# Attention on one core: product 5 of weights and V split into seven smaller products, product 2 split in two of four periods only

## The chip, the cores and the metric

The kernel runs on one core of one Trainium2 chip. The metric is the device time of one execution in microseconds (us); lower is better.

## The reference

For each of 8 batches, with q, k and v of 2048 x 512 in float32:

```python
scores = np.matmul(q, k.transpose(0, 2, 1)) / np.sqrt(d_k)
attn_weights = special.softmax(scores, axis=-1).astype(np.float32)
return np.matmul(attn_weights, v)
```

## The kernel before

**Two products, both by a seven-product scheme.** Both large products (q with k, and the weights exp(scores) with v) are cut into 2 x 2 blocks and made with seven block products in place of eight (the Strassen-Winograd form). The block sums that this needs are additions on VectorE. Operands are float16, sums on TensorE are float32 in PSUM. The softmax has no maximum; exp is taken on ScalarE straight from PSUM, and the row sums come out of an extra column of ones beside v (257 columns in place of 256), so that each output is scaled by a reciprocal at the end.

**Stages.** The work is 32 periods g = 0 to 31, four to each batch; I call g mod 4 the quarter 0 to 3. A period has 28 slots. In each slot one product of q and k is made for the queries of the next two periods (`Group.product`, two matmuls of 512 columns, L317), and between them stand the products of the weights with v for the period's own 2 x 128 query pairs, the "pair" a and the pair b (`Pair.product`, eight matmuls of 256 or 257 columns, L414). The table `ORDER` (L558) says after which slot which product of weights and v stands: "a5" at 10 is product 5 of pair a, "a7'" product 7 of the pair a of the period before. The periods 0, 30 and 31 have orders of their own (`FIRST`, `ALONE`, `LAST`).

**Products 1 and 2 are split once more.** For pairs a and b together, product 1 ("s1" to "s4" in the table) and product 2 ("t1" to "t4") are cut again into seven products of four matmuls with 128 columns each (`fine`, L519). They need sums of weights (`a_sums`, L494 to L497, in the tiles `si`) and of v (`vi_sums`, L241 to L244, once a batch, in `ti`), and within the chain one ScalarE copy of 256 columns from one PSUM bank to another (L527), two ScalarE copies of 128 columns to the output tile (L530, L534) and two VectorE additions (L536, L541). Each later stage ("s2" after "s1") writes columns that the copy has to have read.

**Sums.** `p_sums` (L368 to L371) makes four sums of 128 x 1024 for each pair of a period; a and b have tiles of their own, two buffers each. In the even periods pair a's sums are cut in two (6 of 8 blocks, then 2). `k_sums`, `q_sums` and `v_sums` make the sums of k, q and v for what comes next. `sums_of` (L615) and `KSUMS` (L592) place all of them by slot.

**Outputs.** Each half of a pair's output is a tile of 128 x 512 float32 from a pool of six. ScalarE scales one part (L423), VectorE adds another (L426), and when both 256-column halves are done one DMA of 256 KB stores it from SyncE's queue (L433). The same queue carries the DMA transposes of q and k (L150), in program order. `prefetch` (L601) issues them and the loads.

**Order.** Nothing is scheduled by a tool: every engine works through its instructions in the order in which the program names them, and semaphores hold back what is not ready. Of PSUM's eight banks the pools `qx` (2), `qy`, `qz` (1 each) hold the scores, `px` and `pz` (2 each) the products of weights and v.

Of the kernel before, what the change touches and what calls it, by code (L numbers as in the profile page):

```python
# [12 lines left out]
def kernel(  # L13
# [22 lines left out]
    P = 128  # L36
# [30 lines left out]
    spool = ctx.enter_context(tc.tile_pool(name="spool", bufs=2))  # L67
    opool = ctx.enter_context(tc.tile_pool(name="opool", bufs=6))
# [35 lines left out]
    si = {n: const.tile([P, NI, P], F16, name=f"si{n}") for n in (1, 2, 4)}  # L104
    ti = {}
# [124 lines left out]
    def t3_inner(b):  # L230
        return vi_blocks(b + 1 if b + 1 == B else b)[1]

    def vi_sums(b, s):
        b11, b12, b21, b22 = vi_blocks(b)
        if not ti:
            for n in (1, 2, 4):
                ti[n] = ipool.tile([P, 2, NI, P], F16, tag=f"t{n}", name=f"ti{n}")[:]
        ti[3] = t3_inner(b)
        at = lambda x: x[:, s]
        return [  # L240
            lambda: sub(at(ti[1]), at(b12), at(b11)),  # L241
            lambda: sub(at(ti[2]), at(b22), at(ti[1])),
            lambda: sub(at(ti[3]), at(b22), at(b12)),
            lambda: sub(at(ti[4]), at(b21), at(ti[2])),  # L244
        ]
# [109 lines left out]
    def p_sums(g, which, j0=0, j1=NJ):  # L355

        left, right = pts[g // 2]
        if (g, which) not in psums:
            psums[g, which] = [
                spool.tile([P, NJ, P], F16, tag=f"s{n}", name=f"s{n}") for n in (1, 2, 4)  # L360
            ]
        s1, s2, s4 = psums[g, which]
        cols = columns(g, which)
        js = slice(j0, j1)
        a11, a21 = left[0][:, js, cols], right[:, js, 0, cols]
        a12, a22 = left[1][:, js, cols], right[:, js, 1, cols]
        return [
            lambda: add(s1[:, js], a21, a22),  # L368
            lambda: sub(s2[:, js], s1[:, js], a11),
            lambda: sub(a21, a11, a21),  # L370
            lambda: sub(s4[:, js], a12, s2[:, js]),  # L371
        ]

# [3 lines left out]

    class Pair:

        def __init__(self, g, which):
            self.g, self.which, self.done = g, which, 0

        def product(self, n, j0=0, j1=NJ):
            g = self.g
            left, right = pts[g // 2]
            s1, s2, s4 = psums.get((g, self.which), (None,) * 3)
# [4 lines left out]
            self.apart = g == NP - 1 and alone  # L393
            if n == 1 and j0 == 0:
                self.x = bank("px")
            elif n == 2:
                self.y = bank(own + "y")
            elif n == 5:
                self.z = bank(own + "z")
            lhs, rhs, dst = {  # L400
                1: (lambda j: left[0][:, j, cols], lambda j: vh[:, j, 0, 0:H], "x"),
                2: (lambda j: left[1][:, j, cols], lambda j: vh[:, j, 1, 0:H], "y"),
# [7 lines left out]
            width = H + 1 if n in (3, 5) else H  # L410
            first = n in (1, 2, 5)
# [18 lines left out]
        def store(self, o, half, ds=slice(0, D)):  # L430
            b, sp = divmod(self.g // 2, NSP)
            n = (2 * sp + half) * NT + self.g % 2 * 2 + "ab".index(self.which)
            nc.sync.dma_start(out=out[b, n * P:(n + 1) * P, ds], in_=o[:, ds])  # L433

        def store_first(self):
            self.done += 1
            if self.done == 2:
                self.store(self.o1, 0)

        def after5(self):  # L440
            self.o2 = opool.tile([P, D], F32, tag="o")
            self.r2 = small.tile([P, 1], F32, tag="r2")
            nc.vector.reciprocal(out=self.r2[:], in_=self.z[:, H:H + 1])  # L443
            self.scaled(self.o2[:, H:D], self.z[:, 0:H], self.r2)

        def after3(self):
            self.o1 = opool.tile([P, D], F32, tag="o")
            self.r1 = small.tile([P, 1], F32, tag="r1")
            nc.vector.reciprocal(out=self.r1[:], in_=self.z[:, H:H + 1])
            self.scaled(self.o1[:, 0:H], self.x[:, 0:H], self.r1)  # L450

        def after2(self):
            self.final(self.o1[:, 0:H], self.y[:, 0:H], self.r1)
            self.store_first()

        def after6(self):
            self.scaled(self.o1[:, H:D], self.x[:, 0:H], self.r1)
            self.final(self.o1[:, H:D], self.z[:, 0:H], self.r1)
            self.store_first()

        def after7(self):
            self.final(self.o2[:, H:D], self.x[:, 0:H], self.r2)
            if self.apart:
                self.store(self.o2, 1, slice(H, D))

        def after4(self):
            self.scaled(self.o2[:, 0:H], self.x[:, 0:H], self.r2)
            self.store(self.o2, 1, slice(0, H if self.apart else D))

    class Fine(Pair):  # L470

        def after3(self):
            self.o1 = opool.tile([P, D], F32, tag="o")
            self.r1 = small.tile([P, 1], F32, tag="r1")
            nc.vector.reciprocal(out=self.r1[:], in_=self.z[:, H:H + 1])
            self.scaled(self.o1[:, H:D], self.z[:, 0:H], self.r1)
            self.scaled(self.o1[:, 0:H], self.x[:, 0:H], self.r1)

        def after6(self):
            self.final(self.o1[:, H:D], self.x[:, 0:H], self.r1)
            self.store_first()

    def a_blocks(g, s):
        left = pts[g // 2][0][s]
        ca, cb = columns(g, "a"), columns(g, "b")
        lo, hi = slice(0, NI), slice(NI, NJ)
# [11 lines left out]
    def fine(g, s, stage):  # L500

        a11, a12, a21, a22 = a_blocks(g, s)
        b11, b12, b21, b22 = vi_blocks(g // NQT)
        pa, pb = (pairs.setdefault((g, w), Fine(g, w)) for w in "ab")
        if stage == 1:
            for p in (pa, pb):
                if s == 0:
                    p.x = bank("px")
                else:
                    p.y = bank("pz")  # L510
        xa, xb = (pa.y, pb.y) if s else (pa.x, pb.x)

        def product(n, dst):
            lhs, rhs = {
                1: (a11, b11[:, s]), 2: (a12, b21[:, s]), 3: (si[4], b22[:, s]), 4: (a22, ti[4][:, s]),
                5: (si[1], ti[1][:, s]), 6: (si[2], ti[2][:, s]), 7: (a21, t3_inner(g // NQT)[:, s]),
# [6 lines left out]

        if stage == 1:
            product(1, xb[:, 0:P])
            product(5, xb[:, P:H])
            nc.scalar.copy(out=xa[:, 0:H], in_=xb[:, 0:H])  # L527
        elif stage == 2:
            product(6, xb[:, 0:P])
            nc.scalar.copy(out=pa.o2[:, 0:P], in_=xb[:, 0:P])  # L530
            product(2, xa[:, 0:P])
        elif stage == 3:
            product(7, xb[:, 0:P])
            nc.scalar.copy(out=pa.o2[:, P:H], in_=xb[:, 0:P])  # L534
            product(3, xa[:, P:H])
            nc.vector.tensor_add(xa[:, P:H], xa[:, P:H], pa.o2[:, 0:P])  # L536
            if s:
                pa.after2()
        else:
            product(4, xb[:, 0:P])  # L540
            nc.vector.tensor_add(xb[:, P:H], xb[:, P:H], pa.o2[:, P:H])  # L541
            if s:
                pb.after2()
# [3 lines left out]
    def pv(g, which):  # L547
        if which[0] in "st":
            return fine(g, "st".index(which[0]), int(which[1]))
# [12 lines left out]
    FIRST = "a1< b1< a1> a5 b1> a3 a2 a6 - b5 - b3 b2 b6".split()  # L562
    ALONE = "a7' b7' a4' b4' a1 a5 b1 a3 b5 a6 b3 a2 a7 b6 a4 b2".split()
    LAST = "b7' a1 b4' a5 b1 a3 b5 a6 b3 a2 b6 a7 b7 a4 b2 b4".split()
# [4 lines left out]
    def after_slot(g):  # L569
        order = {0: FIRST, NP - 2: ALONE, NP - 1: LAST}.get(g)  # L570
        if order is None:
            return ORDER
        return {2 * n + 1: x for n, x in enumerate(order) if x != "-"}

    PLAN = {}
    for qt_, slot_, *what_ in (
# [13 lines left out]
    KSUMS = {  # L592
        divmod(slot, NS): (c, n)
        for c, slots in (
            (0, (39, 42, 43, 44)), (1, (56, 59, 60, 65)), (2, (67, 71, 74, 76)), (3, (84, 86, 88, 90))
        )
        for n, slot in enumerate(slots)
    }
    background = deque()

    def prefetch(g, slot):  # L601
# [9 lines left out]
        if (qt, slot) in KSUMS and b + 1 < B:  # L611
            c, n = KSUMS[qt, slot]
            k_sums(c)[n]()

    def sums_of(g, slot):  # L615

        if g == 0:
            return [first_sum(x) for x in SUMS0.get(slot, "").split()]
        todo = []
        b, qt = divmod(g, NQT)  # L620
        inner = g < NP - 2

        def put(slots, items):
            todo.extend(f for at, f in zip(slots, items) if at == slot)

        sp = g // 2 + 1
        if g % 2 == 0 and sp < NP // 2:
            put((2,), q_sums(sp)[2:])
        if g % 2 == 1 and sp + 1 < NP // 2:
            put((24, 26), q_sums(sp + 1))  # L630
        if g % 2 == 0:
            put((4, 4, 5, 5), p_sums(g, "a", NE))
        if inner:
            put((6, 7, 11, 12), a_sums(g, 0))
            put((14, 17, 21, 22), a_sums(g, 1))
        if g % 2 == 0 and sp < NP // 2:
            put((7,), q_sums(sp)[3:])
        put((8, 9, 10, 13) if inner else (7, 9, 11, 13), p_sums(g, "b"))
# [221 lines left out]
```

## Time and profile before

| What | Value |
|---|---|
| Time, median of 3 runs | 795.77 us (795.51 to 795.99) |
| Time of the profiled execution | 795.86 us |
| Its span, first to last instruction | 793.8 us |
| TensorE matmuls (PE) busy | 787.4 us, 99% of the span |
| VectorE (DVE) busy | 678.0 us, 85% |
| ScalarE (ACT) busy | 608.4 us, 77% |
| GpSimd (POOL) busy | 72.3 us, 9% |
| Granted TensorE clock | 1.000 |

The profile has one execution. Its own time is 2.06 us above its span. Rows of it name a line of the kernel, the engine, the operation, output and inputs and shapes; "busy" is the time in which at least one instruction of the engine ran, so that the durations of overlapping instructions add up to more.

### The profile page before, as it was taken

To read this page: it belongs to the slowest core of one execution; us is meant where nothing else is said; L and a number is where in the kernel's file an instruction comes from. 1 tells how busy PE (TensorE), PEld (TensorE's weight loads), DVE (VectorE), ACT (ScalarE), POOL (GpSimd) and SP (SyncE) were. 2 spreads that over 40 slices of the span, in tenths; PEclk is the share of its full clock that TensorE was granted. 3 is DMA by queue.
4 is the path that set the end of the run, shared out by engine and by line. 5 is a ranking of instruction groups with operands and counts; after the bars stand their busy time and mean duration, and the time that the engine had idled before them with its cause. 6 is when DMAs were issued, how large, how long until landed. Compare 5 with 4: busy or idle time off the path is not lost.

```text
span 793.8 us, 16565 instructions
## 1 busy us (share of the span) xinstructions
PE 787.4 (99%) x6226; PEld 537.0 (68%) x6226; DVE 678.0 (85%) x1568; ACT 608.4 (77%) x1194; POOL 72.3 (9%) x106
## 2 busy tenths in 40 slices
PE   9999999999999999999999999999999999999998
PEld 6556666666666666666666666666666666666677
DVE  3789889979899898998989888898888989889773
ACT  4678777877877887778787788878778777778852
POOL 4011010001100010001100111001110101000000
PEclk9999999999999999999999999999999999999999
DMA  9989997989938999389994799667995879911112
GB/s 221 181 147 143 151 179 151 161 136 205 194 65 162 160 200 184 83 152 150 201 163 107 150 152 214 123 135 140 169 206 97 159 137 188 182 41 41 54 55 106
DMA packets 188160, 115.96 MB, mean 146 GB/s; under 512 B 122288, under 2 KB 170800, under 8 KB 188080
## 3 DMA queue, kind: packets, MB, share of 16 engines
q0 software_dynamic: 49648, 49.29, 43.1%
q1 hardware_dynamic: 138144, 65.29, 39.0%
q8 instruction: 48, 0.79, 0.4%
q10 hardware_dynamic: 288, 0.33, 0.1%
q14 instruction: 32, 0.26, 0.1%
HBM read 100.73 MB, written 33.55 MB: 169 GB/s over the span
## 4 chain that ended last, share of the span: by engine, by line
PE 96%; DMA 2%; ACT 1%; DVE 1%; issue 0%; ACTq 0%
PE t L317 45%; PE t L414 36%; PE t L519 11%; PE t L260 2%; DMA kraw<-stage 2%; PE tr L160 1%; PE tr L137 0%; PE t L728 0%; PE t L276 0%; ACT left L253 0%; DVE o L426 0%; ACT o L423 0%; ACT right L253 0%; DVE kraw L163 0%; DVE cz L342 0%
## 5 line engine op out<-in xcount | busy, mean ns | idle before, releaser
L317 PE MATMUL t<-qraw,kraw 128*128 128x512 f16 x728 | 206.4, 379 | 0.1
L414 PEld LDWEIGHTS <-s 128*128 128x128 f16 x1536 | 149.7, 97 | 58.8 <-issue 0.5
L253 ACT ACTIVATE left<-t 128x512 f16<-128x512 f32 (+1 forms) x260 | 156.1, 603 | 22.3 <-PE t L317 16.7
L423 ACT ACTIVATE o<-t,r 128x256 f32<-128x256 f32 x256 | 116.4, 486 | 59.7 <-DVE r L443 32.9
L253 ACT ACTIVATE right<-cz 128x1024 f16<-128x1024 f32 x122 | 129.5, 1061 | 10.0 <-DVE cz L339 9.7
L317 PE MATMUL t<-qs,ks 128*128 128x512 f16 x488 | 135.2, 379 | 0.0
L414 PE MATMUL t<-vt,s 128*128 128x257 f16 (+1 forms) x1024 | 133.8, 273 | 0.0
L414 PEld LDWEIGHTS <-right 128*128 128x128 f16 x1024 | 100.2, 98 | 37.2 <-issue 0.5
L317 PEld LDWEIGHTS <-kraw 128*128 128x128 f16 x976 | 90.3, 98 | 44.3 <-issue 0.6
L426 DVE SCALAR_TENSOR_TENSOR o<-t,r,o 128x256 f32<-128x256 f32 x192 | 92.2, 481 | 27.0 <-PE t L414 11.9
L333 ACT COPY cz<-t 128x512 f32<-128x512 f32 x120 | 70.4, 587 | 47.2 <-PE t L317 45.0
L339 DVE TENSOR_TENSOR cz<-t,cz 128x512 f32<-128x512 f32 x122 | 83.7, 686 | 22.2 <-PE t L317 21.6
L519 PEld LDWEIGHTS <-left 128*128 128x128 f16 x928 | 68.9, 98 | 41.1
L342 DVE TENSOR_TENSOR cz<-t,cz 128x512 f32<-128x512 f32 x122 | 83.8, 687 | 14.6 <-PE t L317 8.3
L317 PEld LDWEIGHTS <-ks 128*128 128x128 f16 x732 | 66.5, 97 | 39.4 <-issue 0.2
L328 ACT COPY t<-t 128x512 f32<-128x512 f32 x120 | 69.0, 575 | 19.2 <-PE t L317 14.9
L317 PE MATMUL t<-qs,kraw 128*128 128x512 f16 x244 | 72.5, 379 | 0.0
L317 PE MATMUL t<-qraw,ks 128*128 128x512 f16 x244 | 72.5, 378 | 0.0
L336 ACT COPY cz<-t 128x512 f32<-128x512 f32 x122 | 71.4, 585 | 0.0
L519 PE MATMUL t<-vh,left 128*128 128x128 f16 x696 | 67.4, 219 | 0.0
L414 PE MATMUL t<-vh,s 128*128 128x257 f16 x512 | 66.9, 272 | 0.2 <-ACT o L423 0.2
L414 PE MATMUL t<-vt,right 128*128 128x256 f16 x512 | 66.2, 273 | 0.3 <-DVE o L426 0.3
(85 smaller groups left out, 937.7 us busy)
## 6 DMA issues: line engine op xcount, KB each, us to landing
out_dram<-o SPq DMA_DIRECT2D x127, 256.0 KB, 3.0
vh<-in_v_dram POOLq DMA_DIRECT2D x32, 512.0 KB, 11.8
stage<-in_q_dram POOLq DMA_DIRECT2D x28, 512.0 KB, 8.2
stage<-in_k_dram POOLq DMA_DIRECT2D x28, 512.0 KB, 7.7
right<-in_q_dram POOLq DMA_DIRECT2D x2, 512.0 KB, 10.2
right<-in_k_dram POOLq DMA_DIRECT2D x2, 512.0 KB, 12.3
first<-in_q_dram SPq DMA_DIRECT2D x2, 256.0 KB, 3.5
cz<-in_q_dram SPq DMA_DIRECT2D x2, 256.0 KB, 4.8
```

The lines of the kernel that those rows point to most:

```text
L253: nc.scalar.activation(out=out_, in_=in_, func=EXP, scale=inv_sqrt_d)
L260: nc.tensor.matmul(st[:], kops[c][0][:, n, dc, :], qraw[0][:, half * NT:(half + 1) * NT, dc, :], start=(dc == 0), stop=(dc == ND - 1),)
L317: nc.tensor.matmul(dst[:], lhs[:, j, dc, :], rhs[:, :, dc, :], start=(n in (1, 5) and dc == 0), stop=(dc == 1), skip_group_check=True,)
L328: f(out=self.y[:], in_=self.x[:])
L333: f(out=self.cz[:, 1, :], in_=self.z[:])
L336: nc.scalar.copy(out=self.cz[:, 0, :], in_=self.x[:])
L339: nc.vector.tensor_add(self.cz[:, 1, :], self.x[:], self.cz[:, 1, :])
L342: nc.vector.tensor_add(self.cz[:, 0, :], self.z[:], self.cz[:, 0, :])
L414: nc.tensor.matmul(dst[:, 0:width], lhs(j), rhs(j), start=(first and j == 0), stop=(j == NJ - 1), skip_group_check=True,)
L423: nc.scalar.activation(out=out_, in_=src, func=COPY, scale=r[:])
L426: nc.vector.scalar_tensor_tensor(out=out_, in0=src, scalar=r[:], in1=out_, op0=MULT, op1=ADD)
L519: nc.tensor.matmul(dst, lhs[:, j, :], rhs[:, j, :], start=(n == 1 and j == 0), stop=(j == NI - 1), skip_group_check=True,)
```

## The change

The core of the diff (new names of variables and the parts that only follow from these are left out):

```diff
-    spool = ctx.enter_context(tc.tile_pool(name="spool", bufs=2))
-    opool = ctx.enter_context(tc.tile_pool(name="opool", bufs=6))
+    spool = ctx.enter_context(tc.tile_pool(name="spool", bufs=1))
+    opool = ctx.enter_context(tc.tile_pool(name="opool", bufs=7))
...
+    ui = {n: const.tile([P, NI, P + 2 if n == 1 else P], F16, name=f"ui{n}") for n in (1, 2, 4)}
+    ti3 = const.tile([P, NI, P], F16, name="ti3")
+    ci = const.tile([P, 2, P], F32, name="ci")
...
     def p_sums(g, which, j0=0, j1=NJ):
-                spool.tile([P, NJ, P], F16, tag=f"s{n}", name=f"s{n}") for n in (1, 2, 4)
+                spool.tile([P, NJ, 2 * P], F16, tag=f"s{n}", name=f"s{n}") for n in (1, 2, 4)
...
-    ORDER = {
-        1: "a7'", 3: "b7'", 5: "a4'", 7: "b4'", 8: "s1", 10: "a5", 11: "s2", 13: "b5", 14: "s3",
-        16: "a3", 17: "s4", 18: "b3", 20: "a6", 21: "t1", 23: "t2", 24: "b6", 25: "t3", 27: "t4",
-    }
+    INNERS = ("xz", "xyz", "xyz", "xz")
+    PRODUCTS = (
+        "a7'@1 b7'@2 a4'@6 u1@8 b4'@9 u2@9 s1@12 u3@12 s2@13 u4@14 s3@15 a3@15 s4@16 b3@18 a6@20 "
+        "a2@22 b6@24 b2@27",
+        "a7'@1 b7'@3 a4'@5 u1@7 b4'@10 u2@10 s1@11 u3@12 s2@13 u4@14 s3@15 a3@16 s4@17 b3@18 "
+        "a6@20 t1@21 t2@23 b6@24 t3@25 t4@27",
+        "a7'@1 b7'@2 a4'@6 u1@8 b4'@9 u2@10 s1@12 u3@12 s2@13 u4@14 s3@15 a3@16 s4@17 b3@18 "
+        "a6@20 t1@20 t2@23 b6@24 t3@25 t4@27",
+        "a7'@1 b7'@2 a4'@6 u1@8 b4'@9 u2@10 s1@12 u3@12 s2@13 u4@13 s3@15 a3@16 s4@17 b3@18 "
+        "a6@20 a2@22 b6@24 b2@26",
+    )
...
+    SUMS = (
+        "v02@0 q3@1 Z3@1 L1@3 z1@4 S2@6 q4@6 z2@7 z4@7 x1@9 z3@10 x3@10 x2@11 v12@11 x4@13 S4@14 "
+        "v03@16 v13@16 N1@16 L3@16 N3@23 v04@24",
+        "v14@0 z1@1 S2@1 z2@3 z4@3 S4@6 Y1@7 z3@8 x1@11 x2@11 x3@12 x4@13 k01@15 y1@16 k03@17 "
+        "k04@17 y2@17 y3@18 k02@19 y4@20 Y2@20 N1@21 Y4@22 Y3@23 N3@24 q1@25 q2@27",
+        "q3@1 L1@4 q4@4 z1@6 S2@6 k11@6 z2@7 L3@8 z4@8 x1@9 z3@10 x2@11 x4@13 k13@14 x3@14 S4@14 "
+        "y1@17 y2@17 k14@17 N1@18 k12@18 N3@20 k21@21 y3@22 k23@23 y4@24 k24@26 k22@27",
+        "z1@0 z2@0 S2@2 z4@2 k31@5 S4@6 z3@7 k33@8 x1@9 x2@11 x3@12 x4@13 X1@13 v01@15 k32@16 "
+        "k34@16 X2@17 X3@17 Z1@17 v11@18 X4@20 Z2@21 Z4@23 N1@23 q1@24 N3@24 q2@27",
+    )
...
         def after2(self):
-            self.final(self.o1[:, 0:H], self.y[:, 0:H], self.r1)
-            self.store_first()
+            if "y" in INNER(self.g):
+                self.final(self.o11, self.y[:, 0:H], self.r1)
+            else:
+                self.o11 = self.half()
+                self.scaled(self.o11, self.y[:, 0:H], self.r1)
+            self.store(self.o11, 0, slice(0, H))
...
         if stage == 1:
             product(1, xb[:, 0:P])
-            product(5, xb[:, P:H])
-            nc.scalar.copy(out=xa[:, 0:H], in_=xb[:, 0:H])
+            product(5, xb[:, P:P + W5])
+            nc.scalar.copy(out=xa[:, 0:P + W], in_=xb[:, 0:P + W])
         elif stage == 2:
             product(6, xb[:, 0:P])
-            nc.scalar.copy(out=pa.o2[:, 0:P], in_=xb[:, 0:P])
+            nc.scalar.copy(out=ci[:, 0], in_=xb[:, 0:P])
             product(2, xa[:, 0:P])
         elif stage == 3:
+            product(3, xa[:, P:P + W])
             product(7, xb[:, 0:P])
...
-                if at == 2 and prev is not None:
-                    prev.exp_right()
+                right = prev if at == 2 else None
...
+            for _ in range(len(later)):
+                later.popleft()()
+            for x in todo.get(slot, ()):
+                pv(g, x)
+            if slot < NS and right is not None:
+                right.exp_right()
```

In words: in the periods 1 to 29 product 5 of both pairs becomes seven products "u1" to "u4" of four matmuls with 128 columns, of which two products carry the column of row sums (129 columns). Their weights are the sums s1 in four blocks, with sums of their own (z1 to z4, L555 to L558 in the new kernel; Z1 to Z4 once a batch for v). Product 2 stays split (t) in the quarters 1 and 2; in the quarters 0 and 3 it is made whole again (a2, b2), and then starts from a ScalarE copy of the bank x into a bank y, and its output is scaled on ScalarE in place of the VectorE addition. The three s tiles hold both pairs with one buffer each, and each sum over weights covers both pairs (S, N, L: 2048, 1536 or 512 elements). Every output half of 256 columns has a tile of its own (seven in the pool; in the last two periods every second one lies in the scores' buffers) and a DMA of 128 KB of its own. Each quarter has an order of its own for products (`PRODUCTS`) and sums (`SUMS`), and the periods 0, 1, 30 and 31 one for sums (`SUMS_AT`). The exponential of the right half now follows the slot's products of weights and v.

More of the change, by code (lines that the diff above doesn't have):

```diff
@@ new lines, in half, with rate @@
+        def half(self):
+            Pair.halves += 1
+            if self.g < NP - 2 or Pair.halves % 2:
+                return opool.tile([P, H], F32, tag="o", name="o")[:]
+            if not spare_halves:
+                t = czpool.tile([P, 2, QH], F32, tag="cz", name="o")
+                spare_halves.extend(t[:, n // 2, n % 2 * H:(n % 2 + 1) * H] for n in range(4))
+            return spare_halves.popleft()
+        def rate(self, tag):
+            r = small.tile([P, 1], F32, tag=tag, name=tag)
+            nc.vector.reciprocal(out=r[:], in_=self.z[:, H:H + 1])
+            return r
@@ L440, in after5 @@
         def after5(self):
[L441 to L444, printed above, removed]
+            self.o22 = self.half()
+            self.r2 = self.rate("r2")
+            self.scaled(self.o22, self.z[:, 0:H], self.r2)
         def after3(self):
-            self.o1 = opool.tile([P, D], F32, tag="o")
-            self.r1 = small.tile([P, 1], F32, tag="r1")
@@ L466, in after4 @@
+            self.store(self.o22, 1, slice(H, D))
         def after4(self):
[L467 to L468 removed]
+            self.o21 = self.half()
+            self.scaled(self.o21, self.x[:, 0:H], self.r2)
+            self.store(self.o21, 1, slice(0, H))
     class Fine(Pair):
[L474 to L479 removed]
+        parts = 0
@@ L590 @@
         PLAN.setdefault((qt_, slot_), []).append(what_)
[L592 to L597, printed above, removed]
-    }
     background = deque()
+    later = deque()
     def prefetch(g, slot):
@@ L684 @@
     nc.gpsimd.memset(vt1[:, :, H:H + 1], 1.0)
+    nc.gpsimd.memset(ui[1][:, :, P:P + 1], 1.0)
     nc.gpsimd.memset(vraw[0][:, :, 1, D:D + 1], 1.0)
-    def row():
-        t = opool.tile([P, D], F32, tag="o", name="first")
-        return t[:]
+    rows = [spool.tile([P, 2, D], F32, tag=f"s{n}", name="first") for n in (1, 2)]
+    rows = [t[:, n] for t in rows for n in range(2)]
     rest = [czpool.tile([P, 2, QH], F32, tag="cz", name="cz") for _ in range(2)]
@@ L807 @@
         todo = after_slot(g)
+        work = placed(SUMS_AT[g] if g in SUMS_AT else SUMS[g % NQT])
         sp = g // 2 + 1
```

291 lines of the change are left out of this document (165 added, 126 removed), and 4 rows, old and new, of the table SUMS0.

## The prediction

> **What bounds the kernel now.** I read the page first, then the busy time by stretches, then the order in time on TensorE, VectorE and ScalarE, then the waits. On the page:
>
> ```profile
> PE 787.4 (99%) x6226; PEld 537.0 (68%) x6226; DVE 678.0 (85%) x1568; ACT 608.4 (77%) x1194; POOL 72.3 (9%) x106
> ...
> PE 96%; DMA 2%; ACT 1%; DVE 1%; issue 0%; ACTq 0%
> ```
>
> TensorE is the chain that ends last. A busy TensorE can hide small gaps, so I look at the stretches (us; then busy time of each engine with its instruction count, granted clock, DMA share, GB/s):
>
> ```profile
> 70.00:118.80 48.80, 48.27 (x389) 32.88 (x387) 41.96 (x101) 38.42 (x77) 5.93 (x8) 1.00 1.15 152
> 118.80:214.90 96.10, 96.10 (x771) 65.60 (x769) 85.62 (x200) 76.75 (x153) 8.90 (x12) 1.00 0.98 166
> ```
>
> From 118.8 us on, one batch (four periods) takes 96.1 us and TensorE never waits. VectorE works 85.6 of it, ScalarE 76.8. Starts in the order of time give what a matmul really costs:
>
> ```profile
> 201.01 1.04 PE L414 MATMUL t<-vt,s 128*128 128x256 f16 x8
> 201.88 0.59 PE L317 MATMUL t<-qraw,kraw 128*128 128x512 f16 x2
> ...
> 214.95 0.39 PE L519 MATMUL t<-ti,si 128*128 128x128 f16 x4
> 215.17 1.03 PE L317 MATMUL t<-qs,ks 128*128 128x512 f16 x4
> 216.04 1.06 PE L414 MATMUL t<-vt,s 128*128 128x257 f16 x8
> 216.93 0.59 PE L317 MATMUL t<-qs,kraw 128*128 128x512 f16 x2
> 217.36 0.39 PE L519 MATMUL t<-ti,si 128*128 128x128 f16 x4
> 217.58 0.39 PE L519 MATMUL t<-vh,left 128*128 128x128 f16 x4
> 217.81 0.59 PE L317 MATMUL t<-qraw,ks 128*128 128x512 f16 x2
> ```
>
> From start to start eight matmuls of 256 columns take 0.87 us, eight of 257 0.89, four of 128 0.22 or 0.23. Averaged over some 300 such rows one matmul costs 215.8 ns (512 columns), 109.2 (256), 111.6 (257), 56.0 (128). A period is then 56 x 215.8 + 48 x 109.2 + 32 x 111.6 + 56 x 56.0 = 24.03 us; measured 96.1 / 4 = 24.03. So columns and instruction counts are the time, with no stall in them.
>
> **Products: the gain.** Product 5 of both pairs is 16 x 111.6 = 1.786 us. Its replacement is 28 matmuls, 20 of 128 and 8 of 129 columns; the extra column I price as from 256 to 257, 2.4 ns. That is 28 x 56.0 + 8 x 2.4 = 1.587: 0.199 saved in each of 29 periods, 5.77 us. Undone splits of product 2 cost 16 x 109.2 - 28 x 56.0 = 0.179 in the 14 periods of quarters 0 and 3 (periods 3 to 28), 2.51 us. Four matmuls of 129 columns in t in 15 periods and 16 of 257 in period 0 cost 0.18. Net -3.08 us, all on the path.
>
> **VectorE.** Costs are again from start to start:
>
> ```profile
> 202.49 0.41 DVE L188 TENSOR_TENSOR ks<-kraw,ks 128x512 f16<-128x512 f16 x1
> 202.82 0.42 DVE L496 TENSOR_TENSOR left<-left 128x512 f16<-128x512 f16 x1
> ...
> 207.96 0.68 DVE L371 TENSOR_TENSOR s<-left,s 128x1024 f16<-128x1024 f16 x1
> 208.56 0.29 DVE L541 TENSOR_TENSOR t<-t,o 128x128 f32<-128x128 f32 x1
> ```
>
> 512 float16 elements cost 0.333 us, 1024 cost 0.600; so 2048 is estimated at 1.134 and 1536 at 0.867. Elsewhere in the same view a scores addition is 0.60, an output addition (L426) 0.40, an addition of 128 floats 0.21, a reciprocal 0.08. Per batch, before: k 5.3, q 4.8, v 4.8, inner v 2.7, weight sums 19.7, inner weight sums 10.7, scores 19.2, outputs 9.6, rest 4.6: 81.4, against 85.6 measured (a factor 1.05 for dependent neighbours). After: inner v 4.0 (Z added), weight sums 18.4 (fewer, wider), inner weight sums 13.3, outputs 8.0 (quarters 0 and 3 lose two each), rest 5.5, others as before: 83.3, so about 87.5 of a batch of 95.7. The heaviest quarter, 2, has 21.85 x 1.05 = 22.9 of 23.85. VectorE stays under TensorE, and by adding up slot for slot I find it at most about 1.5 us behind (2.2 at slot 16 of quarter 0, where v03, v13, N1 and L3 stand together). The scores' addition has three slots until product 4 needs its bank. Cost taken: nothing.
>
> **ScalarE.** u adds copies of 0.37 + 0.14 + 0.14 (L527, L530, L534 from start to start) four times a batch, t drops them twice, the copy x to y adds 4 x 0.37: +2.8, so 79.5 of 95.7. Hidden too, but see the first rival.
>
> **Waits moved.** One buffer for s instead of two: N1 must wait for u4 (slot 13 or 14) and stands at 16 to 23; S2 waits for the last b6 (slot 24) and stands at 1 to 6. Seven half tiles, eight taken per period: the nearest reuse is a tile stored many slots before. Stores double on SyncE's queue (two 128 KB DMAs for one of 256) ahead of the transposes; the queue waits in program order. What hides it is that the k sums move back: k11 from slot 0 of quarter 2 to slot 6, k01 from 11 to 15 of quarter 1. Without that cover the following stall would return:
>
> ```profile
> PE t L519 <- DVE si L497: 0.5, 1, 0.5
> ...
> DVE ks L185 <- DMA kraw<-stage: 1.0, 1, 1.0
> ```
>
> In the first batch VectorE stood 1.0 us at k11 for a transpose, si came late, and TensorE lost 0.69 us (L519 rows at 99.14 and 100.05, less four matmuls). With k11 six slots later (over 5 us) I take this back: -0.69. If the doubled stores made a transpose late in each batch it would be up to 7 x 0.69 = 4.8 on the other side. Period 0 has gaps of 1.0 in all; its orders change, and I take no gain (bounds -1.0 to +1.0). The tail has the same products; the last store was 128 KB already: 0.
>
> **New waits.** The tighter order must cost something; the row to be nearest to is 0 per batch today, the far end is the first rival's 6.3. I take 0.6 (0.02 per period).
>
> Sum against the profiled execution: 795.86 - 3.08 - 0.69 + 0.6 = 792.7; the median of the runs lies 0.09 lower: **792.6 us**.
>
> **Rival 1, slower: the copy inside the small chain comes late.** Stage s2 overwrites columns that ScalarE has to copy first:
>
> ```profile
> 215.43 0.36 ACT L527 COPY t<-t 128x256 f32<-128x256 f32 x1 [0.46 <-PE t L519]
> 215.80 0.59 ACT L333 COPY cz<-t 128x512 f32<-128x512 f32 x1
> ```
>
> s1 issued its last matmul by 215.17; with ScalarE idle the copy ends at 215.79, 0.62 us later. Before, s1 at slot 8 and s2 at 11 had three scores products and a5 between them, 3 x 0.43 + 0.89 = 2.2 us. After, in quarters 0, 2 and 3, only u3 and one scores product: 0.45 + 0.43 = 0.88. That leaves 0.26 for whatever ScalarE is behind. In slots 9 to 11 of quarter 0 it has 0.47 + 0.38 + 0.14 + 0.96 + 0.47 + 0.49 = 2.91 us to do, TensorE 3.07 up to the end of s1: nearly even, and one exp_right that waits for VectorE (it did, up to 1.4 us) uses it up. Price: at 0.3 us in 21 periods 6.3 us: 795.8 - 3.8 + 6.3 = 798.3. It decides against the change from 0.18 us per period on (3.8 / 21). For it: the queue works strictly in order. Against it: exp_right now stands behind the copies of its slot, and before's batches show no stall with a queue 80% full.
>
> **Rival 2, no difference:** the same waits, or a late a3 or t1 behind a VectorE sum of 1.13 us, at 0.08 to 0.13 us in 29 periods: 2.3 to 3.8 eat the gain: 794.3 to 795.8.
>
> **Rival 3, slower: VectorE becomes the bound.** If sums of 2048 float16 elements ran at the rate of float32 additions (0.60 per 512), 12 of 2048 and 4 of 1536 cost 12 x 1.27 + 4 x 0.93 = 19 us more a batch: VectorE at 106, +11 a batch, about 870 in all. No row speaks for it: 1024 cost 0.600 also where L370 reads blocks of 128 out of wider rows.
>
> **Rival 4, slower: long runs of small matmuls.** s1 and u3 make runs of 16, where before had 8. If the second half of a run cost a weight load's mean (L519, 98 ns) in place of 56, it is 8 x 0.042 = 0.34 in 21 periods: 7.1, 799.1. Against it, from the chain of waits in the prologue:
>
> ```profile
> 16.41 0.89 PE tr L160 x16
> ```
>
> 16 with a weight load each at 55.6 ns. The Trainium skill, page "TensorE: Matmul & The Clock Gate", section "Back-to-back issue gap", says that pairs of load and matmul sustain about 81 ns at 128 columns; by that figure (an estimate from the page) each u would cost 28 x 81 = 2.27 us, more than product 5, each t 2.27 against 1.75, and the change would end near 802.6. The trace disagrees: 56.0 ns on every such row.
>
> **How the numbers follow.** Forecast (faster by over 0.2%, below 794.2): 0.60, its own range 791.4 (no new waits, period 0 gains half) to 794.2. Rival 2 and its neighbourhood, within 0.2%: 0.13. Slower: rival 1 0.21, rival 3 0.02, rival 4 0.02, transposes late 0.02, together 0.27. Runs before spread by 0.06%, so that 0.2% (1.6 us) can be told from nothing. The range 791.4 to 798.5 takes in rival 1's price and leaves out about 0.15.
>
> **What would show it.** Right: 128-column matmuls at 56 ns in runs of 16, a batch of 95.7 us with TensorE never idle, VectorE near 87.5 of it, ScalarE near 79.5, no gap at the first k11. Wrong: waits of the small products' line for the copies of ScalarE (rival 1) or for si or s (VectorE late), a batch over 96.1, a 2048 sum above 1.2 us, or a transposed k late in each batch.

## The result, and the profile after

The changed kernel takes 791.12 us (median of ten runs, 790.51 to 792.15); the kernel before, on the same chip, 795.86 (795.16 to 802.77). The ratio is 0.9935, with a 95% interval of 0.9915 to 0.9955: faster, as forecast, and 0.28 us below the low end of the predicted range. The profiled execution took 792.15 us with a span of 790.4; it is the slowest of the ten, and what makes it so lies in the main ahead of period 0 (below).

The page of the changed kernel, busy times and the shares of the chain that ended last:

```profile
PE 783.1 (99%) x6406; PEld 536.7 (68%) x6406; DVE 690.1 (87%) x1508; ACT 629.1 (80%) x1267; POOL 71.8 (9%) x108
...
PE 98%; DMA 1%; ACT 1%; DVE 0%; SPq 0%; issue 0%; ACTq 0%
```

TensorE has 180 matmuls more and is busy 4.3 us less; short stalls count as busy, so this is not the matmuls' work alone. One whole batch, with the columns of the stretch of before (time in the batch, busy TensorE, weight loads, VectorE, ScalarE, GpSimd, granted clock, DMA share, GB/s):

```profile
112.42:208.05 95.63, 95.63 (x794) 65.64 (x792) 87.02 (x193) 79.68 (x163) 8.88 (x12) 1.00 0.92 156
```

TensorE is busy all of it, VectorE 87.02 us and ScalarE 79.68; the prediction had 95.7, 87.5 and 79.5. The small products in the order of time on TensorE (start, duration):

```profile
217.19 0.39 PE L586 MATMUL t<-vh,left 128*128 128x128 f16 x4
217.42 0.39 PE L586 MATMUL t<-ti,si 128*128 128x128 f16 x4
217.65 0.39 PE L586 MATMUL t<-vt,si 128*128 128x129 f16 x4
217.87 0.38 PE L586 MATMUL t<-vt,s 128*128 128x128 f16 x4
218.10 0.59 PE L332 MATMUL t<-qraw,kraw 128*128 128x512 f16 x2
```

In a run of sixteen each group of four still starts 0.22 or 0.23 after the one before, the one with 129 columns too. The groups by shape give the new wide sum (total busy us, mean ns):

```profile
L388 DVE TENSOR_TENSOR s<-left,s 128x2048 f16<-128x2048 f16 x31 | 37.8, 1218 | 0.1
```

1218 ns is the duration; from start to start it is 1.13 us (67.40 to 68.53), the estimate of 1.134. I call a period the time from its first a7' to the next one's; read in the order of time, it is:

| Period | before | changed |
|---|---|---|
| quarter 0 | 24.11 | 24.00 |
| quarter 1 | 24.01 | 23.81 |
| quarter 2 | 24.01 | 23.82 |
| quarter 3 | 24.01 | 24.00 |
| period 0, from the first product of weights and v | 21.82 | 21.25 |
| period 1 | 24.13 | 24.44 |
| period 2 | 24.71 | 23.82 |
| from a7' of period 30 to the start of the last eight matmuls | 28.63 | 28.28 |

From the first product of weights and v to the start of the last eight matmuls (called "the last matmul" from here on), this makes 747.85 us before (41.40 to 789.25) and 742.93 after (42.91 to 785.84): -4.92. By causes: products -3.15; a small gap in quarter 0 of each batch, -0.66; the gap at the first late k sum -0.69; period 0, -0.57; the tail -0.35; new gaps in period 1, +0.50. What lies ahead of period 0 differs by +1.51 in these two executions, what lies behind the last matmul and outside the spans by -0.30, and so the two profiled executions differ by only 3.71. The +1.51 is a late load, in the waits:

```profile
PE tr L140 <- DMA first<-in_k_dram: 1.5, 1, 1.5
```

Its size varies from execution to execution: the first product of weights and v starts at 42.41 in another trace of the changed kernel (below), at 41.17 to 42.24 in variants of it, and at 41.14 to 42.12 in three variants of the kernel before. So the load of the first blocks scatters by over a microsecond in both kernels; whether the changed one tends to start later is not shown. I rest the causes on the traces from period 0 on.

### The profile page after: what moved, and what is told of

It reads as the page before. It is cut to its first block, busy times and chain, and to the rows that moved or that the text cites. A ratio compares the mean times of both kernels' runs of the same rounds, so it can differ in the third digit from the quotient of the medians.

```text
span 790.4 us, 17347 instructions
## 1 busy us (share of the span) xinstructions
PE 783.1 (99%) x6406; PEld 536.7 (68%) x6406; DVE 690.1 (87%) x1508; ACT 629.1 (80%) x1267; POOL 71.8 (9%) x108
## 4 chain that ended last, share of the span: by engine, by line
PE 98%; DMA 1%; ACT 1%; DVE 0%; SPq 0%; issue 0%; ACTq 0%
PE t L332 46%; PE t L437 33%; PE t L586 15%; PE t L275 2%; DMA first<-in_k_dram 1%; PE tr L163 1%; PE t L291 0%; PE tr L140 0%; ACT left L268 0%; ACT right L268 0%; SPq L134 0%; DVE kraw L166 0%; DVE cz L357 0%; ACT cz L348 0%; ACT kraw L142 0%
## 5 line engine op out<-in xcount | busy, mean ns | idle before, releaser
L332 PE MATMUL t<-qraw,kraw 128*128 128x512 f16 x728 | 200.7, 379 | 0.1
L446 ACT ACTIVATE o<-t,r 128x256 f32<-128x256 f32 x256 | 118.5, 477 | 69.1 <-PE t L437 34.6
L268 ACT ACTIVATE left<-t 128x512 f16<-128x512 f32 (+1 forms) x260 | 154.4, 599 | 17.8 <-PE t L332 10.0
L332 PE MATMUL t<-qs,ks 128*128 128x512 f16 x488 | 139.7, 378 | 0.2 <-DVE cz L357 0.2
L437 PEld LDWEIGHTS <-s 128*128 128x128 f16 x1072 | 103.9, 97 | 38.3 <-DVE s L388 1.7
L332 PEld LDWEIGHTS <-kraw 128*128 128x128 f16 x976 | 88.4, 97 | 54.0 <-issue 0.6
L449 DVE SCALAR_TENSOR_TENSOR o<-t,r,o 128x256 f32<-128x256 f32 x164 | 78.1, 480 | 16.8 <-PE t L437 9.0
L586 PEld LDWEIGHTS <-si 128*128 128x128 f16 x876 | 62.7, 97 | 26.7 <-issue 0.2
L437 PE MATMUL t<-vt,s 128*128 128x256 f16 (+1 forms) x560 | 72.5, 273 | 0.0
L437 PE MATMUL t<-vh,right 128*128 128x256 f16 x512 | 66.0, 273 | 0.0
```

Of the source, the lines that this page charges most:

```text
L268: nc.scalar.activation(out=out_, in_=in_, func=EXP, scale=inv_sqrt_d)
L332: nc.tensor.matmul(dst[:], lhs[:, j, dc, :], rhs[:, :, dc, :], start=(n in (1, 5) and dc == 0), stop=(dc == 1), skip_group_check=True,)
L437: nc.tensor.matmul(dst[:, 0:width], lhs(j), rhs(j), start=(first and j == 0), stop=(j == NJ - 1), skip_group_check=True,)
L446: nc.scalar.activation(out=out_, in_=src, func=COPY, scale=r[:])
L449: nc.vector.scalar_tensor_tensor(out=out_, in0=src, scalar=r[:], in1=out_, op0=MULT, op1=ADD)
L586: nc.tensor.matmul(dst, lhs[:, j, :], rhs[:, j, :], start=(n == 1 and j == 0), stop=(j == NI - 1), skip_group_check=True,)
```

## The experiments

The theory after the result: the products are 3.15 us, and the rest is gaps of the kernel before that the changed order closed, each of them a place where TensorE waited for a small piece of work that stood behind others in another engine's fixed order. The rival: what brings the gain is only part of the change (the split of product 5, or the merged sums), and the rest is passenger or loss. Not tried alone are the stores of half the size, the seven half tiles, and the copy x to y in place of a VectorE addition.

**Product 5 whole again** (`e1_fifth_whole`, the changed kernel with u and its sums taken out):

```diff
-        "a7'@1 b7'@2 a4'@6 u1@8 b4'@9 u2@9 s1@12 u3@12 s2@13 u4@14 s3@15 a3@15 ...
+        "a7'@1 b7'@2 a4'@6 a5@8 b4'@9 b5@9 s1@12 s2@13 s3@15 a3@15 ...
```

> The changed kernel with product 5 whole again (a5, b5 at the slots of u1, u2; z and Z sums left out), all else as changed. Theory (TensorE pays by columns and count): 29 x 0.199 = +5.8 us on the changed kernel's 791.1, so about 796.9, above the kernel before, since product 2 stays whole in 14 periods. Rival (the gain comes from the new order, the split itself is eaten by its waits): 791 to 793.

Measured: 810.5 us, ratio 1.0187 (1.017 to 1.0204). Both expectations missed. The periods of a batch are 25.21, 24.36, 24.47 and 24.43 from quarter 0 on: 0.2 us more matmul time in each, and stalls on top. The longest of the waits:

```profile
PE t L587 <- ACT t L602: 6.0, 7, 0.9
```

Seven times, once in each quarter 0, TensorE waited up to 0.9 us at the small products for ScalarE's copy of s1: without u3, a single scores product stands between s1 and s2. Waits for sums of weights on VectorE (`si`), 1.7 and 1.1 us in all, come behind it. In the changed kernel u3 is also what hides that copy, so taking u out in place does not price u.

**Product 5 whole, with the slots of the kernel before** (`e9_fifth_whole_respaced`):

```diff
+        "a7'@1 b7'@3 a4'@5 b4'@7 s1@8 a5@10 s2@11 b5@13 s3@14 a3@16 s4@17 b3@18 "   # all quarters
...
-        ... x1@9 z3@10 x3@10 x2@11 v12@11 x4@13 ...   # quarter 0; the others alike
+        ... x1@6 x3@11 x2@7 v12@11 x4@12 ...
```

> The first run's kernel (product 5 whole) with the slots of the kernel before for s, a5 and b5 (s1 at 8, a5 at 10, s2 at 11, b5 at 13), x sums at 6, 7, 11, 12. Theory (the first run's loss beyond 5.8 us was s2 waiting for the copy of s1, with one scores product between them; spaced out, only the columns are paid): no such waits, periods of 24.01 and 24.19, 796.9. Rival (the loss came from the order of sums): over 800 again.

Measured: 809.69 us, ratio 1.0161 (1.0138 to 1.0185), so the total is the rival's. The waits for the copy of s1 are gone, and quarter 1 now runs without a wait at 24.02 in place of 23.81: 0.21 for u, against the predicted 0.199. The other quarters got new waits (25.80, 24.28 and 24.31 for quarters 0, 2 and 3), of which two are

```profile
PE t L332 <- ACT left L268: 6.4, 7, 0.9
PE t L437 <- ACT t L530: 2.6, 7, 0.4
```

in quarter 0: an exponential and the copy x to y, both late in ScalarE's queue. The price of the split is confirmed in the one quarter where no wait stands beside it. What the whole kernel would take without u and without new waits is not shown: neither of the two arrangements tried reaches it.

**Product 2 split in all four quarters** (`e2_second_split_everywhere`; the sums Y move from quarter 1 to quarter 0):

```diff
-    INNERS = ("xz", "xyz", "xyz", "xz")
+    INNERS = ("xyz", "xyz", "xyz", "xyz")
...
-        "a2@22 b6@24 b2@27",
+        "t1@21 t2@23 b6@24 t3@25 t4@27",
```

> The changed kernel with product 2 split in all four quarters (sums Y moved from quarter 1 to quarter 0, y sums added in quarters 0 and 3). By TensorE's count 14 x 0.179 = -2.5 us: 788.6. VectorE gets 5.2 us a batch more, some 92.7 of 95.3. Rival (VectorE's queue bounds quarters 0 and 3): stalls of over 0.2 us in each of the 14 periods, 791.5 or more.

Measured: 806.84 us, ratio 1.0142 (1.0127 to 1.0157); the rival won. Quarters 1 and 2 stay at 23.81 and 23.82, quarter 3 is 23.98, and quarter 0 takes 26.25. The stretches of one quarter 3 and the quarter 0 behind it (columns as above) show why:

```profile
111.32:135.30 23.98, 23.98 (x206) 16.43 (x204) 22.71 (x55) 19.89 (x42) 0.74 (x1) 1.00 0.51 108
135.30:161.56 26.26, 24.76 (x206) 16.34 (x205) 25.98 (x58) 19.95 (x42) 2.23 (x3) 1.00 0.83 148
```

With the y sums added and the Y sums moved into it, VectorE has 25.98 us to do in a quarter 0 in which TensorE has less than 24 (21.20 in the changed kernel's quarter 0). The profile lists no wait of VectorE there, and so the quarter is as long as VectorE's work. The first of these two waits of TensorE is for a copy after t1 that stands on ScalarE behind 1.16 us of waiting for a reciprocal of VectorE; the second is for VectorE itself:

```profile
PE t L586 <- ACT t L601: 7.1, 7, 1.0
PE t L332 <- DVE cz L354: 2.0, 7, 0.3
```

**Product 2 split in quarter 3 only, besides 1 and 2** (`e8_split_three_quarters`, with the X sums moved to quarter 0, to lighten quarter 3, and two weight sums of period 1 made later, which the diff below leaves out):

```diff
-    INNERS = ("xz", "xyz", "xyz", "xz")
+    INNERS = ("xz", "xyz", "xyz", "xyz")
...
+        "... x1@9 X1@9 z3@10 x3@10 X2@10 x2@11 X3@11 X4@12 x4@13 S4@14 v12@15 ..."   # quarter 0
```

> The changed kernel with product 2 split in quarter 3 too; the sums X moved from quarter 3 to quarter 0 to make room on VectorE there, and in period 1 the sums S2 and S4 moved to slots 6 and 10. By TensorE's count 7 x 0.18 = -1.25, and -0.37 for a gap of period 1: 789.5. VectorE's load then is about 21.6 x 1.05 in quarter 3 and 21.3 x 1.05 in quarter 0, no more than quarter 2 has today. Rival (VectorE's order, not its load, decides, as in the second run): stalls in quarters 3 and 0, 791 or more.

Measured: 804.18 us, ratio 1.0108 (1.0091 to 1.0125). Quarter 3 gains 0.02 (23.98) in place of 0.18, and quarter 0 loses 1.85 (25.84). Here VectorE is busy 23.90 us of one such quarter 0 of 25.83. That would just fit into the 24.00 of the changed kernel, if no sum ever had to wait; here VectorE waits 1.7 us in it for products of TensorE and a copy of ScalarE, and TensorE waits for VectorE's sums. How much of the loss is the order of the sums and how much their amount is not separated. The longest wait:

```profile
PE t L437 <- DVE s L388: 2.9, 7, 0.4
```

So the fourteen periods in which the change leaves product 2 whole are not given away: the predicted 2.51 us of matmul time buy VectorE room in quarters 3 and 0, and in the two arrangements tried a wider split costs 13 and 16 us in all (804.18 and 806.84 less 791.12). Other arrangements of the sums were not tried.

**Sums of the pairs apart** (`e10_sums_of_pairs_apart`) **and the changed kernel again** (`e11_changed_again`), on one chip:

```diff
     def p_sums(g, which, j0=0, j1=NJ):
+        if which == "ab":
+            fa, fb = (p_sums(g, w, j0, j1) for w in "ab")
+            return [lambda n=n: (fa[n](), fb[n]()) for n in range(4)]
```

> The changed kernel with each weight sum over both pairs made as two of half the size, one behind the other. VectorE pays 0.067 us more for each split, about 16 a batch: +1.1 us a batch on 87.5, no wait of TensorE. Theory (VectorE has room of 8%): 791 to 791.6. Rival (its queue is at the edge, as ScalarE's is at the copy of s1): 792.5 or more, with waits for si or s.

> The changed kernel once more, for a second profile. Theory: from period 0 to the end of the span 743.6 us again, and what differs between executions (790.5 to 792.2) lies ahead of period 0, in when the first blocks of q and k land. Rival: the periods themselves differ.

Measured: 791.2 us apart, ratio 0.993 (0.991 to 0.9949); 791.83 for the changed kernel, ratio 0.9935 (0.9915 to 0.9955). The same stretch of each, first the sums apart:

```profile
115.00:305.00 190.00, 190.00 (x1580) 130.77 (x1579) 174.81 (x423) 158.12 (x323) 17.80 (x24) 1.00 0.90 156
```

and the changed kernel again:

```profile
115.00:305.00 190.00, 190.00 (x1578) 130.52 (x1577) 172.72 (x383) 158.48 (x324) 17.80 (x24) 1.00 0.90 155
```

Forty instructions more and 2.09 us of VectorE in two batches, and TensorE has no gap in either. The wide sums save VectorE 1.05 us a batch, for which TensorE waits nowhere in this stretch. In period 1 it does: 24.65 in place of 24.44 with the sums apart, a loss of 0.2 us that the times cannot show. (Period 0 takes 21.66 in place of 21.25, by gaps that lie ahead of its first divided sum and so are not the edit's.) From period 0 to the last matmul the changed kernel takes 742.97 here, 742.93 in the first profile (the 743.6 of the expectation is counted to another end): the periods do not differ between its two profiled executions.

**The copy of s1 made twice** (`e6_copy_of_s1_twice`), to see how much cover the first rival's copy has:

```diff
-            nc.scalar.copy(out=xa[:, 0:P + W], in_=xb[:, 0:P + W])
+            for _ in range(2 if s == 0 else 1):
+                nc.scalar.copy(out=xa[:, 0:P + W], in_=xb[:, 0:P + W])
```

> The changed kernel with ScalarE's 256-column copy after s1 made twice. Theory (margin of 0.04 us in quarters 0, 2 and 3, some 0.4 more in quarter 1): s2 late by about 0.3 us (the copy's cost from start to start) in 21 periods, +6: 797, with waits of the small products' line for the copy. Rival (ScalarE at 80% has room): 791.1.

Measured: 800.09 us, ratio 1.0058 (1.0043 to 1.0073).

```profile
PE t L586 <- ACT t L602: 5.1, 21, 0.3
```

TensorE waits in 21 places by this row (a 22nd stands under another name), and the periods of quarters 0, 2 and 3 grow by 0.39 us (to 24.39, 24.21, 24.39); with period 1, 22 x 0.39 = 8.6. The other periods of quarter 1, where a scores product more lies between, stay at 23.82. The second copy ends 0.39 us after the first, and TensorE pays all of it: in the changed kernel the cover is used up. Its order in time says the same:

```profile
242.08 0.41 ACT L601 COPY t<-t 128x256 f32<-128x256 f32 x1
242.09 0.59 PE L332 MATMUL t<-qraw,kraw 128*128 128x512 f16 x2
242.53 0.38 PE L586 MATMUL t<-ti,si 128*128 128x128 f16 x4
```

The copy ends at 242.49 and s2 starts at 242.53, where it would have started anyway (the row before it takes 0.44 from start to start, as elsewhere). These 0.04 us are not to spare. Where s2 does wait, with the copy made twice, it starts just as long after the copy's end (146.61 + 0.79 = 147.40):

```profile
146.61 0.79 ACT L602 COPY t<-t 128x256 f32<-128x256 f32 x2
147.46 0.38 PE L586 MATMUL t<-ti,si 128*128 128x128 f16 x4 [0.24 <-ACT t L602]
```

And in period 1 of the changed kernel itself the copy is already late:

```profile
74.72 0.59 PE L332 MATMUL t<-qraw,kraw 128*128 128x512 f16 x2
74.81 0.41 ACT L601 COPY t<-t 128x256 f32<-128x256 f32 x1
75.27 0.38 PE L586 MATMUL t<-ti,si 128*128 128x128 f16 x4
```

There s2 starts 0.55 us after the scores product before it, in place of 0.43: 0.12 us lost, once, in both profiles of the changed kernel.

**exp_right ahead of its slot's products** (`e5_exp_right_first`), as before the change:

```diff
-                right = prev if at == 2 else None
+                right = None
+                if at == 2 and prev is not None:
+                    prev.exp_right()
```

> The changed kernel with the exponential of the right half back ahead of its slot's products of weights and v. In the changed kernel's trace s2 starts 0.04 us after ScalarE's copy of s1 ends (copy 242.08 to 242.49, s2 at 242.53), so the cover of the first rival is used up exactly. Theory (any ScalarE idle time ahead of that copy shows up on TensorE): with the exponential earlier ScalarE waits for VectorE's scores addition again as before (up to 1.4 us), and s2 comes late in some periods: 792 to 795. Rival (the place of the exponential does not matter, the sum of work ahead of the copy is the same): 791.1.

Measured: 793.64 us (nine runs), ratio 0.9972 (0.9963 to 0.9982). Quarter 0 takes 24.18 (24.41 in one batch) and quarter 2 23.94 (23.86 in the first batch) in place of 24.00 and 23.82: gaps at s2 of 0.19 and 0.12 in most batches. From period 0 to the last matmul they make 2.2 us, against 1.8 to 2.5 between the medians. So the small move of exp_right behind the copies is what keeps the first rival from coming true in quarters 0 and 2; quarter 3 does not need it (24.00 here too).

**The later loads held back until the second block of k is there** (`e4_gate_on_second_k`; in the changed kernel GpSimd waits for the first), to try the late load of the prologue:

```diff
-    nc.gpsimd.tensor_copy(out=gate[:], in_=firsts["k", 0][:, 0:1])
+    nc.gpsimd.tensor_copy(out=gate[:], in_=firsts["k", 1][:, 0:1])
```

> The changed kernel; GpSimd's first bulk loads wait for the second block of k in place of the first. Theory (the bulk loads overtake that block in some runs and cost 1.5 us in the prologue): runs between 790.4 and 791.3, median 790.7, no gap of 1.5 us before the third group of transposes. Rival (chance of the memory, not of the bulk loads): some runs still near 792.1.

Measured: 791.75 us, ratio 0.9954 (0.9939 to 0.9969). The profiled execution has no late block, but four new gaps of 0.25 to 0.33 at 40.8 to 45.9 us: no gain to be told from the scatter, and no proof of the cause of the late block, which stays open. Two gaps of this kind, 0.30 and 0.33 at 43.1 and 45.1 us, are in the trace of the sums apart (`e10`) too, whose loads wait for the first block, so the edit need not be their cause.

**The gaps of the kernel before, closed in it.** The next three leave the kernel before as it is but for the slots of sums. `e3_before_two_gaps_closed` delays the sums of k's chunk 2 (of its chunks 0 to 3) and the third weight sum of pair b (which then reads a block of weights that has already been replaced, so one of the weight sums of each later period is made from other data):

```diff
-            (0, (39, 42, 43, 44)), (1, (56, 59, 60, 65)), (2, (67, 71, 74, 76)), (3, (84, 86, 88, 90))
+            (0, (39, 42, 43, 44)), (1, (56, 59, 60, 65)), (2, (72, 74, 75, 77)), (3, (84, 86, 88, 90))
...
-        put((8, 9, 10, 13) if inner else (7, 9, 11, 13), p_sums(g, "b"))
+        put((8, 9, 12, 13) if inner else (7, 9, 11, 13), p_sums(g, "b"))
```

> The kernel before with two places moved: the sums k21 to k24 from slots 11, 15, 18, 20 of quarter 2 to 16, 18, 19, 21, and pair b's third weight sum from slot 10 to 12. Theory: the gap of 0.69 us in the first batch and the seven gaps of 0.09 in quarter 0 close, -1.3 us: 794.5. Rival (the gaps have another cause): 795.9 with the gaps in place.

Measured: 795.31 us (ten runs), ratio 0.9993 (0.9984 to 1.0002). The times cannot tell it from no change. The trace can: the 0.69 and all seven gaps of quarter 0 are gone, every period from 2 to 28 is 24.01, and from period 0 to the last matmul it takes 746.48 us (41.14 to 787.62) in place of 747.85: -1.37, expected -1.3. The next two kernels move the same sums of k and not that of pair b: they lose the 0.69 and keep quarter 0 at 24.12, so each of the two gaps has its own sum.

What the gap of quarter 0 is, in the order of time of the kernel before:

```profile
145.71 0.68 DVE L370 TENSOR_TENSOR right<-left,right 128x1024 f16<-128x1024 f16 x1
146.31 0.16 DVE L443 RECIPROCAL r<-t 128x1 f32<-128x1 f32 x1
146.50 0.47 ACT L423 ACTIVATE o<-t,r 128x256 f32<-128x256 f32 x1 [0.47 <-DVE r L443]
146.54 1.06 PE L414 MATMUL t<-vt,s 128*128 128x257 f16 x8
146.88 0.59 ACT L253 ACTIVATE left<-t 128x512 f16<-128x512 f32 x1
147.52 0.59 PE L317 MATMUL t<-qraw,kraw 128*128 128x512 f16 x2
```

A weight sum of 0.60 us holds up the reciprocal, ScalarE waits 0.47 for it, the exponential behind it runs until 147.47, and only then is the bank free in which TensorE makes the next scores product: eight matmuls of 257 columns seem to take 147.52 - 146.54 = 0.98 in place of 0.89. (That it is this bank is read from the order of the rows; that the weight sum sets it off, `e3` shows.)

`e7_before_period0_and_tail` moves the later k sums in the same way, four v sums of period 0 to the slots 18 to 21, and one weight sum of the last periods from slot 25 to 27:

```diff
-                put((20 if g == NP - 2 else 19, 23, 25, 27), p_sums(g + 1, "a"))
+                put((20, 23, 27, 27) if g == NP - 2 else (19, 23, 25, 27), p_sums(g + 1, "a"))
...
-        12: "v20", 14: "b0 v21", 15: "v30", 16: "b1",
-        18: "v31", 19: "b3", 20: "k02", 21: "b2", 22: "A0", ...
+        14: "b0", 16: "b1", 18: "v20",
+        19: "b3 v21", 20: "k02 v30", 21: "b2 v31", 22: "A0", ...
```

> The kernel before with three places moved: k21 to k24 later as in the third run, in period 0 the v sums 2 to 4 of VectorE moved from slots 12 to 18 to slots 18 to 21, and in the last two periods one weight sum from slot 25 to 27. Theory (VectorE's queue in period 0 and at the end holds back a reciprocal and an output addition, on which ScalarE and then TensorE wait): the gaps of 0.82 us around 57 to 66 us, of 0.69 at 99 us and of 0.46 near the end close, up to -1.9 us: 793.9, from period 0 to the end in the trace 1.5 to 1.9 less than before's 748.5. Rival (the gaps are the products' own): 795.2, only the one at 99 us gone.

Measured: 796.59 us (ten runs), ratio 1.0016 (1.0007 to 1.0026): slower, where a gain was expected. The tail's gap is closed (28.18 in place of 28.63), but period 0 takes 22.92 in place of 21.82, with gaps of 0.72 and 0.70 among others, and period 1 24.58 in place of 24.13, with one of 0.57. The theory that the v sums at their old slots hold up period 0 fell: later ones, beside the weight sums of slots 19 and 21, hold it up more.

`e12_before_three_places` keeps the v sums and moves only the weight sum b3 of period 0, from slot 19 to 21, besides the k sums and the tail:

```diff
-        18: "v31", 19: "b3", 20: "k02", 21: "b2", 22: "A0", ...
+        18: "v31", 20: "k02", 21: "b3 b2", 22: "A0", ...
```

> The kernel before with three places moved and all of its products: k21 to k24 as in the third run, one weight sum of the last two periods as in the seventh, and in period 0 pair b's fourth weight sum from slot 19 to 21, behind the reciprocal that waited for it (57.08 us in the profile before). Theory (these places make up what the prediction of the change left out, apart from the 0.09 us of quarter 0): 0.69 + 0.56 + 0.35 = 1.6 us less from the first product of weights and v to the last matmul, 747.85 to 746.2 in the trace; 793.9. Rival (period 0 gains nothing, as in the seventh run): 747 in the trace.

Measured: 795.22 us (ten runs), ratio 0.9998 (0.9989 to 1.0008); the traced stretch 746.79 us (41.63 to 788.42), -1.06 in place of -1.6, between the theory's 746.2 and the rival's 747. Period 0 is 21.45 (-0.37), the k gap is gone (-0.69), the tail 28.18 (-0.45). But period 1 is now 24.50 in place of 24.13:

```profile
PE t L317 <- DVE cz L339: 0.3, 1, 0.3
```

What VectorE puts off in period 0 it seems to owe in period 1. The changed kernel has its new waits in period 1 too, with 24.44; that they are the same debt is not shown.

No version was found that beats the changed kernel by more than the scatter.

## Why the prediction was right or wrong

From period 0 to the last matmul the forecast was -3.08 - 0.69 + 0.6 = -3.17 us, and -4.92 came. Nearly all of the 1.75 between them are gaps of the kernel before that the prediction put at nothing: -0.66 in the quarters 0, -0.57 in period 0, -0.35 in the tail. The terms one by one:

**Products (-3.08): right.** -3.15 by the periods, and u's share of 0.199 is 0.21 in the one quarter where an experiment isolates it.

**The small matmuls at 56 ns: right, and rival 4 did not come.** Runs of sixteen keep 0.22 to 0.23 per four. The 81 ns of the Trainium skill, page "TensorE: Matmul & The Clock Gate", section "Back-to-back issue gap", is not what this kernel pays: by the prediction's estimate from that figure the change would have ended near 802.6, and it measured 791.12.

**The gap in the first batch (-0.69): right in size and cause, wrong in name.** The late sum was the first one of k's chunk 2 (`k21`, moved from slot 11 to 21 of quarter 2), not `k11`. The trace after has no gap there, and in each of the three variants of the kernel before that move these sums (e3, e7, e12) it is closed too.

**"24.03 = 24.03 ... no stall in them": the step that failed most.** I averaged rows from start to start, took 111.6 ns for a matmul of 257 columns, put it back into the sum for the period, and called the agreement proof. The average held the stall: in quarter 0 of every batch the row of 257 columns seems 0.09 us longer, because the product behind it starts late. Without it a period is 24.01, and by that sum a matmul of 257 columns 110.9 ns: (24.01 - 12.08 - 5.24 - 3.14) / 32. Worth -0.66 in all; e3 closes it by moving VectorE's sums and nothing else, and e7 and e12, without pair b's sum among them, do not.

**Period 0 (0) and the tail (0): the same step, a stall put at nothing.** -0.57 and -0.35. The prediction had seen gaps in period 0 and took nothing, and called the tail's products the same, without following which wait ended last in either. The kernel before, in the order of time of period 0:

```profile
56.48 0.68 DVE L371 TENSOR_TENSOR s<-left,s 128x1024 f16<-128x1024 f16 x1
57.08 0.16 DVE L443 RECIPROCAL r<-t 128x1 f32<-128x1 f32 x1
57.27 0.47 ACT L423 ACTIVATE o<-t,r 128x256 f32<-128x256 f32 x1 [1.18 <-DVE r L443]
57.80 1.04 PE L414 MATMUL t<-vh,s 128*128 128x257 f16 x8 [0.20 <-ACT o L423]
```

and the changed kernel:

```profile
57.73 0.16 DVE L469 RECIPROCAL r<-t 128x1 f32<-128x1 f32 x1
57.81 0.67 DVE L388 TENSOR_TENSOR s<-left,s 128x1024 f16<-128x1024 f16 x1
57.93 0.47 ACT L446 ACTIVATE o<-t,r 128x256 f32<-128x256 f32 x1 [0.34 <-DVE r L469]
```

The reciprocal now stands ahead of the weight sum, and ScalarE waits 0.34 in place of 1.18. The two gaps that TensorE had from there on in period 0, 0.37 at 57.80 and 0.21 at 58.88, are both gone, and they make up the -0.57; one ahead of them, 0.13 at 56.14, is left as 0.14 at 57.64. That this order is the cause is shown in part: moving b3 alone in the kernel before brings 0.37 (e12). In the tail a gap of 0.46 at 773.56 (products of weights and v behind VectorE's L426) is gone, which a weight sum two slots later also does (e7, e12).

**New waits (+0.6, as 0.02 per period): right in sum by luck, wrong in place.** +0.50, all in period 1; the periods 2 to 29 have none:

```profile
70.67 1.02 PE L332 MATMUL t<-qs,ks 128*128 128x512 f16 x4 [0.21 <-DVE cz L357]
```

TensorE stands 0.37 us there for VectorE's addition of scores. The rest is 0.12 at s2 and 0.10 before the second half of u3's run, less 0.12 that the kernel before lost in its period 1.

**Rival 1: the mechanism exists and the place was read rightly; it came in one period of the 22.** In period 1 it costs 0.12 us, in the 21 periods of quarters 0, 2 and 3 nothing, and two experiments bring it about there (e5, e6). The price of 0.3 us per period had no row behind it: the exponential in its old place costs 0.12 to 0.19 in two quarters, one copy more 0.39 in three. The 0.26 us that I saw left for ScalarE to be behind is used up whole. **Rival 3: out**, with the wide sums at 1.13 us. But VectorE is nearer to the bound than 87.02 of 95.63 sounds. Quarter 2 has 22.94 to 23.06 of 23.82, as predicted (22.9 of 23.85), and 4.8 us of additions more in quarter 0 made it the bound there (e2).

**The low end of the range (791.4)** took no new waits and half of the gain in period 0, in a kernel that I held to be without stalls otherwise. It left out the gaps of quarter 0 and of the tail; their 1.0 us would have covered the result. By its own terms (792.6 - 0.6 - 0.5) that low end is 791.5, not 791.4.

## What to carry to other kernels

When rows are averaged from start to start, look at the largest too: a stall that returns once in a batch is inside the mean, and a sum that uses the mean cannot show it. On engines that work through a fixed order, ask of each small instruction for which another engine waits (here a reciprocal of 0.16 us) what long one stands ahead of it; its delay can go through ScalarE's queue to TensorE. An engine that is busy 91% of a batch can be at 97% in one quarter of it, so price what is added by the quarter, and ask in which period a delay is paid.

## What the runs showed of the hardware

Unexpected was how hard the edge is: s2 starts 0.05 us after the end of ScalarE's copy both where it loses nothing (the 21 periods of quarters 2, 3 and 0) and where it waits, and a copy more that ends 0.39 us later costs 0.39 in each. And the load of the first blocks moved the start of period 0 by up to 1.7 us between executions and variants (41.17 to 42.91 for the changed kernel and its variants), which no experiment explained.
